# Two small fp32 products of a two-layer token-mixing trunk made from rounded parts: the GLA gate's product in one stacked pass, the heads' mean squares in two passes

## The chip, the cores and the metric

One core of one Trainium2 chip. The metric is the device time of one execution in microseconds (us), the median of three runs.

## The reference, cut to what matters

Two layers over 512 positions of width 1024. Each layer has a token mixer and a convolutional feed-forward part. The mixer projects the normalised input once, runs three groups of heads of width 64 (6 retention, 6 stick-breaking, 4 gated linear attention, "GLA") and projects their outputs. The two products that the change touches are the GLA gate and the mean squares over the 64 columns of a head:

```python
def head_groupnorm(o, g):
    ...
    mu = jnp.mean(o, axis=-1, keepdims=True)
    var = jnp.mean(jnp.square(o - mu), axis=-1, keepdims=True)
    return (o - mu) * lax.rsqrt(var + EPS) * g...
def head_rmsnorm(o, g):
    ...
    return o * lax.rsqrt(jnp.mean(o * o, axis=-1, keepdims=True) + EPS) * g...
def token_mixer(hn, w_in, gla_w2, gla_b, ret_norm_g, gla_norm_g, w_out):
    ...
    ret = merge_heads(head_groupnorm(ret, ret_norm_g)) * jax.nn.silu(rg)
    ...
    log_alpha = jax.nn.log_sigmoid(glr @ gla_w2 + gla_b) / GLA_TAU   # glr: 16 columns
    ...
    go = merge_heads(head_rmsnorm(go, gla_norm_g)) * jax.nn.silu(gg)
    return jnp.concatenate([ret, sb, go], axis=-1) @ w_out
```

All of it is fp32.

## The kernel before, in words

**Products.** Nearly every large product is fp32 made of three passes of a rounded type (fp32r): each operand is split into a rounded part "hi" and the rest "lo", and `mm3` adds hi x hi, hi x lo and lo x hi in PSUM. A weight's split is in `unit`: a DMA into `raw`, ScalarE's cast to `hi` (L361), VectorE's subtraction to `lo` (L362). `split` (L372, L373) does the same for an intermediate result. All matmuls pass through one helper, so their line is L92.

**The mixer of a layer** consists of pieces that are interleaved: the projections of 128 columns (24 fp32r matmuls of 128x512 each, tiles `pj`), a chain for the two GLA pairs of heads, a chain that alternates the three stick-breaking pairs and the three retention pairs (order s0 r0 s1 r1 s2 r2), and steps of the conditioning vector ("ada", L255 on VectorE, one DMA each), which in layer 0 run beside the mixer. A string of letters per layer (TOK) fixes the order in which the program issues pieces. A scheduler makes each engine's final order at build time out of that order and its own account of which inputs will be ready; each engine then runs its own list in that order, and the lists are what the rows of the order below show. The matmuls of `head_rstd` are under `seq("n")` with mode 0, which leaves their place to the scheduler.

**The gate's product.** `use_gv` (L564) takes the 16 columns of the low-rank projection, transposes them to `glrT` (16 x 512) and loads `gla_w2` into `w2` (16 x 256). `gla_pair` multiplies 16x128 of `w2` with `glrT` as one fp32 matmul: two pairs and two layers make four of them. ScalarE and VectorE make the gate from it, and the seven levels of the pair's scores (groups of 32 products of 64x64) follow.

**The mean squares.** `normed` squares a 128x512 output of two heads on ScalarE (L436); `head_rstd` multiplies it with the constant `blk64` (1/64 in two diagonal blocks) as one fp32 matmul (L423 by way of L92) and makes the reciprocal root: Ln and Exp (L226), a correction step (L429 square on ScalarE, L430 on VectorE, L431 on ScalarE), then L439 and L440 on VectorE. Three retention pairs and two GLA pairs in each of two layers make ten of these products.

**A pair of stick-breaking heads** (`sb_head`) starts with scores on TensorE; then, for three tiles, Abs (L780), Exp, Ln, a cast (L785) on ScalarE and two steps on VectorE (L783, L786); more products; Exp. **A retention pair** makes its scores in the same way, multiplies them with decays on VectorE (L827), adds up values on TensorE, and ScalarE copies the result out (L834).

**The end of the mixer.** The last retention pair's and the second GLA pair's mean squares stand next to each other; behind them on TensorE come the matmuls of the output projection `wo`, which begin with the stick-breaking heads' columns, and on ScalarE five Silu gates (L867) between two table loads, and then the first split (L372) of a gated output.

Of the kernel before, what the change touches and what calls it, by code (L numbers as in the profile page):

```python
# [12 lines left out]
F32R = mybir.dt.float32r  # L13
# [3 lines left out]
ALU = mybir.AluOpType  # L17
AX = mybir.AxisListType

P = 128  # L20
S = 512
# [77 lines left out]
def trunk(ctx: ExitStack, tc: tile.TileContext, A, out, dbg=None):  # L99
# [18 lines left out]
    def nm(s):  # L118
        cnt[0] += 1
        return f"{s}_{cnt[0]}"  # L120

    def T(tag="m", shape=(P, 512), dt=F32):
        tag = TMAP.get(tag, tag)
        return tiles[tag].tile(list(shape), dt, tag=tag, name=nm(tag + "_"))
# [4 lines left out]
    def bank(t):  # L129
        t = PMAP[t]  # L130
        return banks[t].tile([P, 512], F32, tag=t, name=nm(t))
# [4 lines left out]
    def psz():  # L136
        return bank("pz")
# [4 lines left out]
    def psg():  # L142
        return bank("pg")

    V, SC, G, PE = nc.vector, nc.scalar, nc.gpsimd, Recorder(nc.tensor)

    @contextmanager
    def seq(kind):

        mode = MODE[kind]  # L150
        m = (None, PE.last, PE.lastp)[mode]
        if m is not None:
            with tc.issue_after(m.ins):
                yield
        else:
            yield
        if kind == "p":
            PE.lastp = PE.last

    lastw = [None]  # L160
    start = {"on": True, "ld": None, "pe": None, "ws": []}

    def ld(t, src, gated=False, kind=None):
        q = QUEUE.get(kind, "sp")
        if q != "sp":
            return (G if q == "g" else SC).dma_start(t, src)


        m = lastw[0] if gated else start["ld"]
        if m is None:  # L170
            r = nc.sync.dma_start(t, src)
        else:
            with tc.issue_after(m.ins):
                r = nc.sync.dma_start(t, src)
        if start["on"]:
            start["ld"] = r
        return r
# [5 lines left out]
    def as32(t):  # L183
        return t.bitcast(F32)


    def const(name, shape, dt=F32, kind=None):
        t = cp.tile(list(shape), dt, tag=name, name=name)
        ld(t, A[name], False, kind)
        return t  # L190
# [33 lines left out]
    def act(*a, **k):  # L224
        with tc.issue_after(tables[0].ins):
            last_act[0] = SC.activation(*a, **k)  # L226
# [143 lines left out]
    def split(ps, th="m", tl="m"):  # L370
        h, l_ = T(th, dt=F32R), T(tl, dt=F32R)
        SC.copy(h, ps)  # L372
        V.tensor_tensor(l_, ps, as32(h), ALU.subtract)  # L373
        return h, l_
# [44 lines left out]
    def head_rstd(sq):  # L419

        ps = psg()
        with seq("n"):
            PE.matmul(ps, C["blk64"], sq, start=True, stop=True)  # L423
        y = T("hl")
        act(y, ps, AF.Ln, bias=epsc, scale=1.0)
        act(y, y, AF.Exp, scale=-0.5)

        t = T("hl")
        SC.activation(t, y, AF.Square)  # L429
        V.scalar_tensor_tensor(t, ps, EPS, t, ALU.add, ALU.mult)  # L430
        SC.activation(t, t, AF.Copy, bias=1.5, scale=-0.5)  # L431
        return y, t

    def normed(o, gcol):
        sq = T("hl")
        SC.activation(sq, o, AF.Square)  # L436
        yield
        y, t = head_rstd(sq)
        V.scalar_tensor_tensor(o, o, gcol, y, ALU.mult, ALU.mult)  # L439
        V.tensor_tensor(o, o, t, ALU.mult)  # L440
# [6 lines left out]
    C = {}  # L447
# [3 lines left out]
    V.memset(C["reset"].rearrange("p (c t) -> p c t", t=CH)[:, :, 0:1], 0.0)  # L451

    def late_consts():
        for n in ("tri", "negones"):
            t = T("hl", (P, P))
            ld(t, A[n])
            C[n] = cp.tile([P, P], F32R, tag=n, name=n)
            V.tensor_copy(C[n], t)
        t = T("hl", (P, P))
        ld(t, A["negm"])  # L460
        C["negm"] = cp.tile([P, P], BF16, tag="negm", name="negmb")
        V.tensor_copy(C["negm"], t)
        C["identb"] = cp.tile([P, P], BF16, tag="identb", name="identb")
        V.tensor_copy(C["identb"], ident)
        C["blk64"] = const("blk64", (P, P))
        C["lev"] = const("lev", (P, len(LEVELS), CH), U32)
        pv[1] = cp.tile([P, NPV], F32, tag="pv1", name="pv1")
        ld(pv[1], A["pv"][1])
# [74 lines left out]
    def mixer(l, hnh, hnl, after):  # L543
# [3 lines left out]
        res = {}  # L547
# [16 lines left out]
        def use_gv(tb, ps):  # L564
            vtok[tb] = T("gv", (P, 272))
            SC.copy(vtok[tb], ps[:, 0:272])
            if tb == NTB - 1:
                w2 = T("gl", (16, 256))
                ld(w2, A["gla_w2"][l], True)
                ps = psg()  # L570
                for t in range(NTB):
                    PE.transpose(ps[0:16, t * P : t * P + P], vtok[t][:, 256:272], ident)
                glrT = T("gl", (16, S))
                SC.copy(glrT, ps[0:16, :])
                res["w2"], res["glrT"] = w2, glrT

        trig, dms = [], {}

# [14 lines left out]
        def project(n):  # L593
            if n[:2] in ("sv", "gv", "rv"):
                src, w, use = {"sv": (A["wsv"], 384, use_sv), "gv": (A["wgv"], 272, use_gv),
                               "rv": (A["wrv"], 384, use_rv)}[n]
                if n in start:
                    for tb, ps in enumerate(start.pop(n)):
                        use(tb, ps)
                else:  # L600
                    yield from proj_tok(src[l], w, hnh, hnl, use)
                res[n] = True
                return
            res[n] = project_T(n[:2], int(n[2]))
            yield
# [284 lines left out]
        for tb in range(NTB):  # L890
            cs = slice(tb * P, tb * P + P)
            ps = psz()
# [76 lines left out]
    if WARM:  # L969

        ps = psz()
# [78 lines left out]
    start["sv"], start["T"] = acc, accT  # L1050
    start["on"] = False
    late_consts()
    crow_d = dp.tile([1, D], F32, tag="crow", name="crow")
    ld(crow_d.rearrange("o (k p) -> (o k) p", p=P), crow)
# [113 lines left out]
```

## Time and profile before

| what | value |
|---|---|
| median of 3 runs | 1392.14 us (1389.92 to 1395.08) |
| the profiled execution's own time | 1393.45 us |
| its span, first to last instruction | 1391.7 us |
| TensorE (PE) busy | 1354.5 us, 97% of the span |
| VectorE (DVE) / ScalarE (ACT) busy | 838.3 us, 60% / 633.3 us, 46% |
| mean granted TensorE clock | 0.995 of full speed |
| fp32r matmuls of the projections | 976 x 3, 392 ns each as recorded |

The recorded time of a matmul is longer than the step from one start to the next, because they overlap in the pipeline; where a matmul's cost is wanted, the starts are compared. A fp32 matmul shows as two records (x2).

### The profile page before, as it was taken

To read this page: it belongs to the slowest core of one execution; us is meant where nothing else is said; L and a number is where in the kernel's file an instruction comes from. 1 tells how busy PE (TensorE), PEld (TensorE's weight loads), DVE (VectorE), ACT (ScalarE), POOL (GpSimd) and SP (SyncE) were. 2 spreads that over 40 slices of the span, in tenths; PEclk is the share of its full clock that TensorE was granted. 3 is DMA by queue.
4 is the path that set the end of the run, shared out by engine and by line. 5 is a ranking of instruction groups with operands and counts; after the bars stand their busy time and mean duration, and the time that the engine had idled before them with its cause. 6 is when DMAs were issued, how large, how long until landed. Compare 5 with 4: busy or idle time off the path is not lost.

```text
span 1391.7 us, 19758 instructions
## 1 busy us (share of the span) xinstructions
PE 1354.5 (97%) x7619; PEld 1110.6 (80%) x7619; DVE 838.3 (60%) x1572; ACT 633.3 (46%) x1033; POOL 54.0 (4%) x97
## 2 busy tenths in 40 slices
PE   8999999999999999999999999999999999999997
PEld 5887667767988888888899877777898888888886
DVE  4559988665888874424563587776565444443232
ACT  5455465765543333322254556675564333332220
POOL 1000000001000000000020000000010000000000
PEclk9999999999999999999999999999999999999999
DMA  9635461204677852233753222111343223222233
GB/s 323 222 119 170 156 210 59 77 32 165 233 254 254 260 187 100 91 105 119 241 172 123 69 92 76 46 62 61 122 151 113 99 92 106 91 98 100 91 106 106
DMA packets 73999, 186.22 MB, mean 134 GB/s; under 512 B 8833, under 2 KB 9905, under 8 KB 73905
## 3 DMA queue, kind: packets, MB, share of 16 engines
q1 hardware_dynamic: 72512, 182.68, 38.9%
q0 software_dynamic: 1088, 2.12, 0.4%
q8 instruction: 60, 0.98, 0.3%
q14 instruction: 35, 0.28, 0.1%
q10 hardware_dynamic: 304, 0.16, 0.1%
HBM read 176.51 MB, written 8.41 MB: 133 GB/s over the span
## 4 chain that ended last, share of the span: by engine, by line
PE 65%; DVE 5%; ACT 3%; DMA 1%; issue 1%; POOL 0%; DVEq 0%; POOLq 0%; SPq 0%; ACTq 0%
PE pj L92 40%; PE ps L92 25%; DVE lo L362 1%; ACT hi L361 1%; DMA m__707_3526<-x 0%; DMA m__1755_9280<-x 0%; DMA raw<-wu 0%; DMA raw<-wT 0%; ACT junk L516 0%; ACT junk L307 0%; POOL s L295 0%; DVE hnl L342 0%; ACT m__1632_8684 L226 0%; DVE m__1675_8921 L742 0%; DVE m__1460_7779 L742 0%
## 5 line engine op out<-in xcount | busy, mean ns | idle before, releaser
L362 DVE TENSOR_TENSOR lo<-raw,hi 128x1024 fp32r<-128x1024 f32 (+2 forms) x208 | 245.7, 1183 | 258.2 <-ACT hi L361 250.0
L92 PE MATMUL pj<-hnh,lo 128*128 128x512 f32 x976 | 382.3, 392 | 2.0 <-DVE lo L362 2.0
L92 PE MATMUL pj<-hnh,hi 128*128 128x512 f32 x976 | 383.6, 393 | 0.0
L92 PE MATMUL pj<-hnl,hi 128*128 128x512 f32 x976 | 382.1, 392 | 0.0
L361 ACT CAST hi<-raw 128x1024 fp32r<-128x1024 f32 (+2 forms) x208 | 211.5, 1018 | 334.9 <-PE pj L92 171.0
L92 PEld LDWEIGHTS pj<-hnh,lo 128*128 128x128 f32 x976 | 183.7, 188 | 40.5 <-DVE lo L362 2.3
L92 PEld LDWEIGHTS pj<-hnh,hi 128*128 128x128 f32 x976 | 183.7, 188 | 39.7 <-issue 2.8
L92 PEld LDWEIGHTS pj<-hnl,hi 128*128 128x128 f32 x976 | 183.6, 188 | 37.7 <-issue 0.8
L255 DVE SCALAR_TENSOR_TENSOR ada<-ada,cB 128x512 f32<-128x512 f32 x160 | 107.2, 686 | 32.1 <-DMA ada<-ada 31.1
L92 PE MATMUL pj<-hi,hnh 128*128 128x384 f32 (+1 forms) x160 | 51.2, 320 | 0.0
L92 PE MATMUL pj<-lo,hnh 128*128 128x384 f32 (+1 forms) x160 | 50.9, 318 | 0.0
L92 PE MATMUL pj<-hi,hnl 128*128 128x384 f32 (+1 forms) x160 | 50.9, 318 | 0.0
L295 POOL TENSOR_TENSOR s<-s,nhalf 128x1 f32<-128x1 f32 x32 | 20.4, 638 | 760.0 <-DVE s L293 756.4
L92 PE MATMUL ps<-hnl,hi 128*128 128x256 f32 x128 | 36.4, 288 | 1.1 <-DVE hnl L342 1.1
L92 PE MATMUL ps<-hnh,lo 128*128 128x256 f32 x128 | 35.8, 284 | 0.0
L92 PE MATMUL ps<-hnh,hi 128*128 128x256 f32 x128 | 35.8, 289 | 0.0
L524 ACT ACTIVATE junk<-ps 128x512 bf16<-128x512 f32 x16 | 9.6, 597 | 51.5 <-PE ps L92 51.3
L92 PEld LDWEIGHTS pj<-hi,hnh 128*128 128x128 f32 x160 | 30.1, 188 | 0.5
L92 PEld LDWEIGHTS pj<-lo,hnh 128*128 128x128 f32 x160 | 30.0, 188 | 0.3
L92 PEld LDWEIGHTS pj<-hi,hnl 128*128 128x128 f32 x160 | 30.1, 188 | 0.0
L92 PEld LDWEIGHTS ps<-hnl,hi 128*128 128x128 f32 x128 | 24.6, 193 | 1.5 <-DVE hnl L342 1.3
L92 PEld LDWEIGHTS ps<-hnh,hi 128*128 128x128 f32 x128 | 24.7, 197 | 0.0
(2786 smaller groups left out, 2485.5 us busy)
## 6 DMA issues: line engine op xcount, KB each, us to landing
raw<-wu SPq DMA_DIRECT2D x88, 512.0 KB, 3.3
ada<-ada SPq DMA_DIRECT2D x160, 256.0 KB, 3.5
raw<-wd SPq DMA_DIRECT2D x44, 512.0 KB, 3.2
raw<-wT SPq DMA_DIRECT2D x42, 512.0 KB, 3.5
raw<-wo SPq DMA_DIRECT2D x16, 512.0 KB, 3.2
raw<-wsv SPq DMA_DIRECT2D x8, 384.0 KB, 3.6
raw<-wrv SPq DMA_DIRECT2D x8, 384.0 KB, 3.1
raw<-wgv SPq DMA_DIRECT2D x8, 272.0 KB, 2.7
```

Of the source, the lines that this page charges most:

```text
L92: self.last = self.e.matmul(*a, **k)
L255: V.scalar_tensor_tensor(raw, raw, 1.0, cB[h], ALU.mult, ALU.mult, accum_out=pt[:, 4 * h + j : 4 * h + j + 1])
L295: G.tensor_tensor(r, v, nhalf, ALU.pow)
L361: SC.copy(h, raw)
L362: V.tensor_tensor(l_, raw, as32(h), ALU.subtract)
L524: SC.activation(junk, ps, AF.Square, accum_out=ss)
```

## The change

The gate's product becomes one fp32r matmul over 128 rows. Two tiles are filled with zeros by GpSimd. `w3` holds the rounded `gla_w2` at partitions 0 and 64 and its rest at 32; `g3` holds the rounded `glrT` at 0 and 32 and its rest at 64, so that one pass adds hi x hi, lo x hi and hi x lo. Per layer this adds two memsets on GpSimd, two copies of 16x256 and two subtractions on VectorE, and one more copy of 16x512 on ScalarE.

The mean squares' product becomes two fp32r passes with the rounded square and its rest. Each of the ten gets a cast (L372, ScalarE) and a subtraction (L373, VectorE) of 128x512. `blk64` is now loaded with `tri` and `negones` through a staging tile and a copy.

```diff
@@ head_rstd
         with seq("n"):
-            PE.matmul(ps, C["blk64"], sq, start=True, stop=True)
+            for i, t in enumerate(split(sq)):
+                PE.matmul(ps, C["blk64"], t, start=(i == 0), stop=(i == 1))
@@ late_consts
-        for n in ("tri", "negones"):
+        for n in ("tri", "negones", "blk64"):
...
-        C["blk64"] = const("blk64", (P, P))
@@ use_gv
-                w2 = T("gl", (16, 256))
+
+                w2, w3, g3 = T("gl", (16, 256)), T("gl", (P, 256), F32R), T("gl", dt=F32R)
+                for t in (w3, g3):
+                    G.memset(as32(t), 0.0)
                 ld(w2, A["gla_w2"][l], True)
+                for r in (0, 64):
+                    V.tensor_copy(w3[r : r + 16, :], w2)
+                V.tensor_tensor(w3[32:48, :], w2, as32(w3[0:16, :]), ALU.subtract)
                 ps = psg()
                 for t in range(NTB):
                     PE.transpose(ps[0:16, t * P : t * P + P], vtok[t][:, 256:272], ident)
-                glrT = T("gl", (16, S))
-                SC.copy(glrT, ps[0:16, :])
-                res["w2"], res["glrT"] = w2, glrT
+                for r in (0, 32):
+                    SC.copy(g3[r : r + 16, :], ps[0:16, :])
+                V.tensor_tensor(g3[64:80, :], ps[0:16, :], as32(g3[0:16, :]), ALU.subtract)
+                res["w2"], res["glrT"] = w3, g3
```

Lines of the changed kernel are one higher from the product in `head_rstd` up to the constants, and seven higher behind `use_gv` (L436 is L437 there, L780 is L787). The scheduler also gives other places to instructions that the diff does not touch.

**First place: TensorE and VectorE at the mean squares of retention pair 0 in layer 0.** In a row stand line, operation, tile written <- tiles read, and shape. `pj_...` is a projection, `ps_1822` (now `ps_1832`) the mean squares, `ps_1833` to `ps_1835` (now `ps_1848` to `ps_1850`) the scores of stick-breaking pair 1. TensorE before:

```order
L92 MATMUL pj_2016<-hnh_116,hi_2012 128x512
L95 MATMUL ps_1745<-ident,m__334_1736 128x128 x4
L92 MATMUL ps_1822<-m__331_1712,blk_654 128x512
L92 MATMUL ps_1833<-m__276_1471,m__313_1641 128x512
L92 MATMUL ps_1833<-m__278_1473,m__313_1641 128x512
```

TensorE now, behind the same transposes, one matmul of `pj_2031` and 20 of `pj_1919` that read `lo_1916` or come after such a one:

```order
L92 MATMUL pj_1919<-hnl_117,hi_1915 128x512
L92 MATMUL pj_1919<-hnh_116,lo_1916 128x512
L92 MATMUL ps_1832<-m__361_1833,blk_650 128x512
L92 MATMUL ps_1848<-m__278_1481,m__315_1651 128x512
L92 MATMUL ps_1848<-m__280_1483,m__315_1651 128x512
L92 MATMUL ps_1849<-m__278_1481,m__315_1651 128x384
L92 MATMUL ps_1849<-m__280_1483,m__315_1651 128x384
L92 MATMUL ps_1850<-m__278_1481,m__315_1651 128x256
L92 MATMUL ps_1850<-m__280_1483,m__315_1651 128x256
L92 MATMUL ps_1849<-m__278_1481,m__315_1651 128x128
L92 MATMUL ps_1832<-m__362_1834,blk_650 128x512
```

VectorE before:

```order
L399 SCALAR_TENSOR_TENSOR m__351_1799<-m__347_1791,m__349_1797 64x512
L399 SCALAR_TENSOR_TENSOR m__352_1800<-m__347_1791,m__350_1798 64x512
L362 TENSOR_TENSOR lo_2013<-raw_2010,hi_2012 128x1024
L255 SCALAR_TENSOR_TENSOR ada_1940,s_1809<-ada_1940,cB_110 128x512
L740 COPY m__339_1752<-ps_1943 64x64 x2
```

VectorE now:

```order
L399 SCALAR_TENSOR_TENSOR m__353_1809<-m__349_1801,m__351_1807 64x512
L399 SCALAR_TENSOR_TENSOR m__354_1810<-m__349_1801,m__352_1808 64x512
L362 TENSOR_TENSOR lo_2028<-raw_2025,hi_2027 128x1024
L373 TENSOR_TENSOR m__362_1834<-m__333_1722,m__361_1833 128x512
L255 SCALAR_TENSOR_TENSOR ada_1955,s_1819<-ada_1955,cB_110 128x512
```

The product of the mean squares stood right behind the transposes; its first pass now stands behind 22 projection matmuls (the 24 of `pj_1919` but for the two that stand ahead of the transposes), the second behind seven of the scores. The new subtraction (L373) stands behind the long L362. The cast that it reads (`m__361_1833`) stands on ScalarE behind the two L398 of the pair's queries.

**Second place: TensorE and ScalarE at the end of the mixer of layer 0.** `ps_3083` and `ps_3094` (now `ps_3108` and `ps_3124`) are the last two mean squares, of GLA pair 1 and of retention pair 2, `ps_3138` (now `ps_3173`) the first tile of the output projection. TensorE before:

```order
L92 MATMUL ps_3083<-m__589_3032,blk_654 128x512
L92 MATMUL ps_3094<-m__604_3081,blk_654 128x512
L92 MATMUL ps_3138<-hi_3144,m__286_1520 128x512
L92 MATMUL ps_3138<-lo_3145,m__286_1520 128x512
L92 MATMUL ps_3138<-hi_3144,m__287_1521 128x512
```

TensorE now:

```order
L92 MATMUL ps_3108<-m__614_3109,blk_650 128x512
L92 MATMUL ps_3108<-m__615_3110,blk_650 128x512
L92 MATMUL ps_3124<-m__619_3125,blk_650 128x512
L92 MATMUL ps_3173<-hi_3179,m__288_1530 128x512
L92 MATMUL ps_3173<-lo_3180,m__288_1530 128x512
L92 MATMUL ps_3173<-hi_3179,m__289_1531 128x512
L92 MATMUL ps_3124<-m__620_3126,blk_650 128x512
```

ScalarE before:

```order
L834 COPY m__603_3079<-ps_3070 128x512
L436 ACTIVATE m__604_3081<-m__603_3079 128x512
L226 ACTIVATE m__606_3085<-ps_3083,epsc 128x512
L226 ACTIVATE m__606_3085<-m__606_3085 128x512
L429 ACTIVATE m__607_3088<-m__606_3085 128x512
L226 ACTIVATE m__609_3096<-ps_3094,epsc 128x512
L226 ACTIVATE m__609_3096<-m__609_3096 128x512
L431 ACTIVATE m__607_3088<-m__607_3088 128x512
```

ScalarE now:

```order
L841 COPY m__611_3104<-ps_3095 128x512
L437 ACTIVATE m__612_3106<-m__611_3104 128x512
L372 CAST m__614_3109<-m__597_3057 128x512
L226 ACTIVATE m__616_3115<-ps_3108,epsc 128x512
L226 ACTIVATE m__616_3115<-m__616_3115 128x512
L430 ACTIVATE m__617_3118<-m__616_3115 128x512
L372 CAST m__619_3125<-m__612_3106 128x512
L432 ACTIVATE m__617_3118<-m__617_3118 128x512
L226 ACTIVATE m__621_3131<-ps_3124,epsc 128x512
```

The cast for the second product (`m__619_3125`) has come to stand behind Ln, Exp and the square (L430) that the first product's result goes through, and TensorE has the second product's first pass ahead of the output projection.

**Third place: TensorE at the mean squares of retention pair 1 in layer 0.** Before, the product follows the 32 small products of a GLA level. Now the last of the small products is followed by 11 projection matmuls, the last of which stands first here:

```order
L92 MATMUL pj_2817<-hnh_116,lo_2814 128x512
L92 MATMUL ps_2627<-m__520_2628,blk_650 128x512
L92 MATMUL ps_2643<-m__433_2226,m__441_2269 128x512
L92 MATMUL ps_2643<-m__435_2228,m__441_2269 128x512
L92 MATMUL ps_2644<-m__433_2226,m__441_2269 128x384
```

Ahead of the small products stand 14 projection matmuls that before stood behind them: the scores of stick-breaking pair 2 (`ps_2643` to `ps_2645`) have moved behind 25 matmuls of 128x512.

## Rows read from the trace of the kernel before

**Rows 1.** The page of the profile: the span, the first line of part 1 (busy time of each engine, its share of the span, its instructions) and the first line of part 4 (share of the chain of waits that ended last, by engine).

```profile
span 1391.7 us, 19758 instructions
...
PE 1354.5 (97%) x7619; PEld 1110.6 (80%) x7619; DVE 838.3 (60%) x1572; ACT 633.3 (46%) x1033; POOL 54.0 (4%) x97
...
PE 65%; DVE 5%; ACT 3%; DMA 1%; issue 1%; POOL 0%; DVEq 0%; POOLq 0%; SPq 0%; ACTq 0%
```

**Rows 2.** The timeline of TensorE at the first gate product of layer 0. Columns: start in us, busy us, engine, line, operation, tile written <- tiles read, shape, and in brackets the idle time just before it with what ended it.

```profile
84.38 0.39 PE L92 MATMUL pj<-hnh,lo 128*128 128x512 f32 x1
84.69 1.12 PE L92 MATMUL ps<-m__163_870,m__161_863 16*128 16x512 f32 x2
...
86.08 0.40 PE L92 MATMUL pj<-hnl,hi 128*128 128x512 f32 x1
```

**Rows 3.** The timeline of TensorE at the mean squares of retention pair 0 in layer 1; same columns.

```profile
844.37 0.40 PE L92 MATMUL pj<-hnh,hi 128*128 128x512 f32 x1
844.60 1.12 PE L92 MATMUL ps<-m__1456_7769,blk 128*128 128x512 f32 x2
...
845.79 0.39 PE L92 MATMUL ps<-m__1416_7577,m__1442_7695 128*128 128x512 f32 x1
```

**Rows 4.** The timeline of TensorE around the mean squares of retention pair 0 in layer 0; same columns.

```profile
157.53 0.63 PE L95 MATMUL ps<-ident,m__334_1736 128*128 128x128 f32 x4 [0.23 <-DVE m__334_1736 L709]
157.99 1.02 PE L92 MATMUL ps<-m__331_1712,blk 128*128 128x512 f32 x2
...
160.41 0.50 PE L92 MATMUL pj<-hnh,lo 128*128 128x512 f32 x1
...
165.32 0.39 PE L92 MATMUL pj<-hnh,lo 128*128 128x512 f32 x1
...
169.24 0.50 PE L92 MATMUL pj<-hnh,lo 128*128 128x512 f32 x1 [2.01 <-DVE lo L362]
```

**Rows 5.** The timeline of ScalarE (ACT) at the same place; same columns.

```profile
163.49 1.29 ACT L398 ACTIVATE m__349_1797<-m__347_1791 64x512 fp32r<-64x512 f32 x2 [4.71 <-DVE m__347_1791 L590]
164.79 1.28 ACT L398 ACTIVATE m__350_1798<-m__347_1791 64x512 fp32r<-64x512 f32 x2
166.10 0.69 ACT L226 ACTIVATE m__359_1824<-ps,epsc 128x512 f32<-128x512 f32 x1
```

**Rows 6.** The timeline of VectorE (DVE) at the same place; same columns.

```profile
159.14 1.22 DVE L362 TENSOR_TENSOR lo<-raw,hi 128x1024 fp32r<-128x1024 f32 x1
...
167.96 1.23 DVE L362 TENSOR_TENSOR lo<-raw,hi 128x1024 fp32r<-128x1024 f32 x1
```

**Rows 7.** The timeline of TensorE at the mean squares of retention pair 1 in layer 0: the 32 small products of the GLA level just before them; same columns.

```profile
243.71 0.69 PE L92 MATMUL ps<-m__499_2528,m__498_2527 64*64 64x64 f32 x32
```

**Rows 8.** The timeline of ScalarE there, from the square of retention pair 1 to the first step of stick-breaking pair 2; same columns.

```profile
243.11 0.63 ACT L436 ACTIVATE m__502_2544<-m__501_2542 128x512 f32<-128x512 f32 x1
...
247.61 0.39 ACT L780 ACTIVATE m__519_2633<-ps 128x256 f32<-128x256 f32 x1
...
251.16 1.05 ACT L361 CAST hi<-raw 128x1024 fp32r<-128x1024 f32 x1 [0.78 <-PE pj L92]
```

**Rows 9.** [...]

```profile
169.83:173.24 3.41, 3.41 (x10) 2.61 (x8) 3.33 (x9) 1.91 (x4) 0.00 (x0) 0.50 0.64 231
247.60:272.10 24.50, 23.29 (x175) 18.56 (x173) 14.79 (x25) 19.20 (x35) 1.04 (x2) 1.00 0.16 55
272.10:282.40 10.30, 7.71 (x42) 6.17 (x44) 7.82 (x13) 7.26 (x13) 1.00 (x2) 1.00 0.25 93
282.47:285.88 3.41, 3.41 (x18) 1.55 (x16) 2.10 (x8) 0.00 (x0) 0.00 (x0) 0.50 0.48 159
```

**Rows 10.** The timeline of TensorE at the end of the mixer of layer 0, from the last mean squares into the output projection; columns as in Rows 2.

```profile
296.06 1.13 PE L92 MATMUL ps<-m__604_3081,blk 128*128 128x512 f32 x2 [0.28 <-ACT m__604_3081 L436]
296.62 0.79 PE L92 MATMUL ps<-hi,m__286_1520 128*128 128x512 f32 x1
...
306.73 0.50 PE L92 MATMUL ps<-hi,m__611_3112 128*128 128x512 f32 x1
```

**Rows 11.** The timeline of ScalarE at the same place; same columns.

```profile
295.38 0.63 ACT L436 ACTIVATE m__604_3081<-m__603_3079 128x512 f32<-128x512 f32 x1
295.92 0.67 ACT L226 ACTIVATE m__606_3085<-ps,epsc 128x512 f32<-128x512 f32 x1
296.62 0.63 ACT L226 ACTIVATE m__606_3085<-m__606_3085 128x512 f32<-128x512 f32 x1
297.28 0.63 ACT L429 ACTIVATE m__607_3088<-m__606_3085 128x512 f32<-128x512 f32 x1
...
306.06 0.62 ACT L372 CAST m__611_3112<-m__411_2092 128x512 fp32r<-128x512 f32 x1
```

**Rows 12.** The timeline of VectorE at the end of the mixer of layer 1: one subtraction of a split; same columns.

```profile
978.86 0.69 DVE L373 TENSOR_TENSOR m__1705_9057<-m__1509_8057,m__1704_9056 128x512 fp32r<-128x512 f32 x1 [0.83 <-ACT m__1704_9056 L372]
```

**Rows 13.** The timeline of TensorE at the end of the mixer of layer 1; same columns.

```profile
966.77 1.13 PE L92 MATMUL ps<-m__1688_8994,blk 128*128 128x512 f32 x2
968.22 1.12 PE L92 MATMUL ps<-m__1697_9025,blk 128*128 128x512 f32 x2 [0.32 <-ACT m__1697_9025 L436]
968.78 0.79 PE L92 MATMUL ps<-hi,m__1419_7596 128*128 128x512 f32 x1
...
978.88 0.50 PE L92 MATMUL ps<-hi,m__1704_9056 128*128 128x512 f32 x1
```

## The prediction

> **What bounds the kernel now.** The page comes first: TensorE is busy 1354.5 of 1391.7 us, and it has 65% of the chain of waits [rows 1]. So a microsecond of matmul taken away is a microsecond won, as long as TensorE then has something ready; some 37 us of idle time is all there is. Next the timeline of TensorE shows what the two products cost. Then the stretches: in the mixer of layer 0 TensorE is not full everywhere. [...] The change takes work from TensorE and puts two steps, a cast and a subtraction, in front of each mean square; so the question is at each of the ten places what TensorE does until they are done, and the order of the engines answers it.
>
> **Part 1, the gate's product, four times.** From the projection matmul before it to the second one behind it the starts lie 86.08 - 84.38 = 1.70 us apart [rows 2]. Projection matmuls follow each other at 4.91 / 21 = 0.23 us, 22 of them from 160.41 to 165.32 [rows 4]. So the product costs 1.70 - 2 x 0.23 = 1.24 us. One rounded pass of 512 columns costs 0.23, with some 0.06 that a change of destination may add (84.38 to 84.69 is 0.31): 0.95 us saved, **4 x 0.95 = 3.8 us**. What is added beside it (memsets, copies of 16 rows, one subtraction) belongs to the first pair's preparation, with whole projections between it and its use; I cost it at nothing. Without that cover, the chain of one copy and one subtraction would cost about 1.3 us a layer.
>
> **Part 2, the mean squares, ten times.** 845.79 - 844.37 - 2 x 0.23 = 0.96 us for the fp32 product [rows 3], against two passes at 0.46: 0.50 us saved, **10 x 0.50 = 5.0 us**. The two passes are seen to cost 0.23 at this very shape, so I leave no wide bound here. [...] Together: **-8.8 us** if nothing waits.
>
> **Part 3, retention pair 0 of layer 0.** Behind the transposes (157.53 + 0.46) and one matmul, TensorE comes to `lo_1916` at 158.2; the subtraction that writes it runs from 159.14 [rows 6], and the first matmul that needed it started at 160.41 [rows 4]. Before, the mean squares and the scores filled that time; now they stand behind: 2.2 us idle. 22 matmuls later, at 165.5, the first pass needs its cast, which stands on ScalarE behind L398, over at 164.79 + 1.28 = 166.07 [rows 5]; with 0.62 for the cast, as at 306.06 [rows 11], 166.7: 1.2 us idle. The second pass, at 168.1, needs the subtraction behind the L362 that starts at 167.96 and takes 1.14 until the next can start; with 0.69 for itself [rows 12] it is there at 169.8: 1.7 us. That makes 5.1. The 2.01 us that TensorE waited at 169.24 [rows 4] go, since that operand is now there in time. **+3.1 us.** Bounds: nothing, if VectorE gets to its work earlier; 5.1.
>
> **Part 4, retention pair 1 of layer 0.** 14 matmuls now come ahead of the small products that started at 243.71 [rows 7]: 246.9. These take 0.6, two more matmuls end a projection at 248.1, and there ScalarE gets its next weight's cast (1.05 [rows 8]), a copy of about 0.6 and then the cast of the square: 250.3. TensorE arrives at 250.1. Scores and passes take about 2, Ln, Exp and the square 2.0 [rows 11]: the Abs of stick-breaking pair 2, at 247.61 before [rows 8], comes at about 254.2, 6.6 us later, while TensorE has done 25 x 0.23 = 5.8 us of its filling work beforehand. If that chain can't be shortened, the end of the mixer moves by 6.6; if TensorE sets the pace again, by nothing. Over the stretch TensorE was busy 92% [rows 9], and the chain waited for it in places; I take the middle, **+3.5 us**.
>
> **Part 5, the ends of the two mixers.** Layer 0: the square of the last output is done at 296.0, the cast of the first comes behind it, 295.92 to 296.5 [rows 11]. Pass one at 296.6, subtraction to 297.2, pass two to 297.7. Then ScalarE's Ln, Exp and square, 0.70, 0.66 and 0.54 from start to start: 299.6. Only there the second cast can start, to 300.2, and pass one of the second product stands on TensorE ahead of the output projection, whose first matmul thus starts at 300.5, against 296.62 [rows 10]. The gated output that TensorE took at 306.73 is then ready at about 310.1, by the same steps, and wanted at 310.6, so no new wait arises there. **+3.9 us.** For layer 1 the same order from 966.77 gives the output projection at 972.65 against 968.78 [rows 13], again +3.9. Since 1.0 of the savings of part 2 lie in each, this is 4.9 of waiting each, **+9.8 us**. The rule behind it: an instruction whose inputs are ready waits when one ahead of it on its engine does. The Ln at 166.10 shows it: its product was made from 157.99 on, and it started when the L398 ahead of it were over [rows 4, 5]. [...] If ScalarE could take the cast earlier instead, this part would be +0.9 each and the whole change would be faster.
>
> **Part 6, the other four products** (GLA pair 0 in both layers, retention pairs 0 and 1 in layer 1) are also moved, behind 11 to 35 projection matmuls, so that cast and subtraction are mostly covered; what is late next is the start of a stick-breaking or GLA chain, by 2 to 3 us, with less filling work left. Nearest row: part 3, 3.1. Bounds 0 and 3.1 each; I take 0.7, because in layer 1 no ada steps stand ahead: **+2.8 us**.
>
> **Sum.** -8.8 + 3.1 + 3.5 + 9.8 + 2.8 = **+10.4 us**. The profiled execution (1393.45, of which 1391.7 is the span) is 1.3 above the median; put on the median 1392.1 this gives **1402.5 us**, slower by 0.75%.
>
> **Rivals.**
> - *Faster: TensorE stays the bound.* The waits are taken up by projection matmuls, as 97% busy suggests, and the saving remains: 1392.1 - 8.8 = 1383.3. It decides the case if the waits add up to less than 1.8 us, since 8.8 - 1.8 = 7 us (0.5%) is about what a measurement of this kernel can tell from no change. For it: the share of 97% [rows 1]. Against it: at the ends no other matmul stands between the passes. 0.11.
> - *No change: ends only.* Parts 3, 4 and 6 are covered, the ends are not: -8.8 + 9.8 = +1, 1393; up to part 3 with it, 1396. 0.25.
> - *Much slower: the late chains.* Parts 4 and 6 at their upper bounds: -8.8 + 3.1 + 6.6 + 9.8 + 12.4 = +23, 1415; a further half-clock stretch of 3.41 us, as the two in [rows 9], costs 1.7 each. 0.12.
> - *The rounded passes cost what the fp32 product costs*, and nothing is saved: 1411. The rows of 0.23 speak against it; within the slower cases, 0.02.
>
> **The numbers.** Forecast and its neighbours (1399 to 1412) 0.50, with the two slower rivals 0.64 for slower by over 0.5%; same 0.25; faster 0.11. The range 1387 to 1413 leaves out the faster case and the top of the slowest.
>
> **What would show it.** Right: in the changed profile the output projection of each mixer starts about 4 us later behind the last stick-breaking or retention values than before, TensorE idle between two passes of mean squares there; idle before L92 `lo` and two waits for L372 and L373 at retention pair 0; gate products with one record of 0.39. Wrong: TensorE's busy time falls by about 9 and its idle time does not grow, or the idle time grows elsewhere than at these casts and subtractions.

## The result, and the profile after

| | before | changed |
|---|---|---|
| median of 5 runs | 1392.47 us | 1413.38 us (1412.66 to 1416.01) |
| ratio | | 1.0141, 95% interval 1.012 to 1.0163 |
| span of the profiled execution | 1391.7 us | 1414.2 us |
| mean granted clock there | 0.995 | 0.98 |

Slower by 1.4%, some 20 us; the forecast was slower by 10. The median of these five, 1413.38, is 0.4 us above the 1413 at which the stated range ends; the ratio put on the forecast's 1392.1 us gives 1411.7, inside its top. The execution that was profiled is the slowest of the five (1416.01; its clock of 0.98 is the lowest, the others have 0.982 to 0.987), so its trace shows somewhat more than the median. The page of the changed kernel, lines as in [rows 1]:

```profile
span 1414.2 us, 19802 instructions
...
PE 1366.9 (97%) x7615; PEld 1124.4 (80%) x7615; DVE 848.0 (60%) x1591; ACT 639.4 (45%) x1045; POOL 55.3 (4%) x101
...
PE 56%; DVE 8%; DMA 6%; ACT 3%; issue 1%; POOL 0%; DVEq 0%; POOLq 0%; ACTq 0%; SPq 0%
```

TensorE has less to do and is busy 12.4 us *longer*; its share of the chain of waits fell from 65% to 56%, VectorE's rose from 5% to 8% and that of DMA from 1% to 6%. These shares don't tell where the time went: DMA's new share is the conditioning vector's transfers in layer 0's feed-forward part, and what lies between the two mixers is only 1.2 us longer. Where it happened is seen in two stretches of either kernel, each up to the first matmul of an output projection: the mixer of layer 0 from 140 us on, and all from the start of the feed-forward part's last product in layer 0 (its first 126 us are the same in all these traces) to layer 1's output projection. The columns, as in [rows 9], are the stretch and its length in us, the busy us and the instructions of PE, PEld, DVE, ACT and POOL, TensorE's granted clock as a share of full speed, the DMA share and GB/s. Before:

```profile
140.00:296.62 156.62, 144.59 (x1041) 107.71 (x1040) 124.73 (x263) 88.80 (x151) 6.55 (x12) 0.98 0.35 115
593.88:968.78 374.90, 368.81 (x2316) 301.53 (x2314) 227.29 (x427) 186.14 (x320) 18.65 (x31) 1.00 0.32 107
```

Changed:

```profile
140.00:309.22 169.22, 149.82 (x1041) 114.14 (x1040) 129.45 (x270) 92.74 (x158) 6.75 (x12) 0.91 0.32 106
607.72:991.11 383.39, 372.64 (x2312) 305.67 (x2311) 232.90 (x438) 190.50 (x328) 19.36 (x33) 0.99 0.31 104
```

Layer 0: 156.62 to 169.22, +12.6 us; TensorE is idle 19.4 us in place of 12.0 (length less busy time) and busy 5.2 longer at a mean clock of 0.91. Layer 1: +8.5; idle 10.75 in place of 6.09. Together 21.1 of the 22.5 us by which the spans differ; what follows each mixer is nearly as long as before. The half-clock stretches (granted 0.50 or 0.51 of full speed) in the mixer of layer 0, of which before there were two of 3.41 us [rows 9]:

```profile
160.63:164.04 3.41, 3.41 (x8) 2.76 (x9) 3.39 (x7) 0.37 (x1) 0.00 (x0) 0.51 0.95 330
181.02:191.25 10.23, 10.10 (x47) 8.66 (x48) 7.69 (x17) 5.01 (x10) 0.00 (x0) 0.50 0.84 266
279.97:293.60 13.63, 7.07 (x30) 4.92 (x31) 7.51 (x16) 5.68 (x10) 0.99 (x2) 0.50 0.16 60
307.30:314.10 6.80, 5.48 (x13) 4.37 (x14) 3.39 (x5) 4.75 (x8) 0.00 (x0) 0.50 0.00 0
```

34 us at half clock, and TensorE busy in 26 of them. In the second TensorE was busy but for 0.13 us, and no idle time just ahead of it is longer than 0.73; the first, third and fourth lie behind or around idle time of 2.02, 5.67 and 2.61 us, shown below.

### The profile page after: what moved, and what is told of

Same layout as the page of the kernel before. It is cut to its first block, busy times and chain, and to the rows that moved or that the text cites. A ratio compares the mean times of both kernels' runs of the same rounds, so it can differ in the third digit from the quotient of the medians.

```text
span 1414.2 us, 19802 instructions
## 1 busy us (share of the span) xinstructions
PE 1366.9 (97%) x7615; PEld 1124.4 (80%) x7615; DVE 848.0 (60%) x1591; ACT 639.4 (45%) x1045; POOL 55.3 (4%) x101
## 4 chain that ended last, share of the span: by engine, by line
PE 56%; DVE 8%; DMA 6%; ACT 3%; issue 1%; POOL 0%; DVEq 0%; POOLq 0%; ACTq 0%; SPq 0%
PE pj L92 32%; PE ps L92 25%; DMA ada<-ada 6%; DVE lo L362 2%; DVE ada L255 1%; ACT hi L361 1%; DMA m__719_3561<-x 0%; DMA m__1823_9538<-x 0%; DMA raw<-wT 0%; DVE hnl L342 0%; DVE m__1340_7120 L708 0%; DVE m__1694_8979 L749 0%; DVE m__1472_7821 L749 0%; DVE m__1473_7822 L749 0%; DVE s L558 0%
## 5 line engine op out<-in xcount | busy, mean ns | idle before, releaser
L362 DVE TENSOR_TENSOR lo<-raw,hi 128x1024 fp32r<-128x1024 f32 (+2 forms) x208 | 245.7, 1183 | 249.0 <-ACT hi L361 245.8
```

Of the source, the lines that this page charges most:

```text
L362: V.tensor_tensor(l_, raw, as32(h), ALU.subtract)
```

## The places of the prediction, in the trace after

The first gate product, TensorE, columns as in [rows 2]:

```profile
85.58 0.39 PE L92 MATMUL pj<-hnh,lo 128*128 128x512 f32 x1
85.81 0.39 PE L92 MATMUL ps<-m__164_867,m__163_866 128*128 128x512 f32 x1
86.04 0.39 PE L92 MATMUL pj<-hnh,hi 128*128 128x512 f32 x1
```

One record, and the next matmul starts 0.23 us later, as far apart as the projection's pass before it (85.58) and the product (85.81): the product costs what a projection's pass costs, 0.06 less than forecast.

Retention pair 0 in layer 0, TensorE, to set against [rows 4]:

```profile
157.71 0.63 PE L95 MATMUL ps<-ident,m__336_1746 128*128 128x128 f32 x4 [0.24 <-DVE m__336_1746 L716]
...
160.59 0.80 PE L92 MATMUL pj<-hnh,lo 128*128 128x512 f32 x1 [2.02 <-DVE lo L362]
...
167.30 0.40 PE L92 MATMUL ps<-m__361_1833,blk 128*128 128x512 f32 x1
167.53 0.39 PE L92 MATMUL ps<-m__278_1481,m__315_1651 128*128 128x512 f32 x1
...
168.84 0.50 PE L92 MATMUL ps<-m__362_1834,blk 128*128 128x512 f32 x1
```

The wait of 2.02 us for `lo` stands where it was expected (2.2). The other two, for the cast and the subtraction, do not: TensorE, at half clock from 160.63 to 164.04 (granted 0.51), came to its first pass at 167.30 and found the cast done. The run ends_fp32 (below) has the same order here, and in its trace the clock is full at this place (granted 1.00 from 158 to 163 us); there all three waits come, the last two at 1.03 and 0.21 us (forecast 1.2 and 1.7):

```profile
158.94 0.50 PE L92 MATMUL pj<-hnh,lo 128*128 128x512 f32 x1 [2.02 <-DVE lo L362]
...
165.30 0.50 PE L92 MATMUL ps<-m__361_1833,blk 128*128 128x512 f32 x1 [1.03 <-ACT m__361_1833 L372]
...
167.13 0.50 PE L92 MATMUL ps<-m__362_1834,blk 128*128 128x512 f32 x1 [0.21 <-DVE m__362_1834 L373]
```

Retention pair 1 in layer 0, ScalarE, from the new cast to the Abs of stick-breaking pair 2, to set against [rows 8]:

```profile
250.08 0.62 ACT L372 CAST m__520_2628<-m__508_2564 128x512 fp32r<-128x512 f32 x1
252.97 0.69 ACT L226 ACTIVATE m__522_2634<-ps,epsc 128x512 f32<-128x512 f32 x1 [2.27 <-PE ps L92]
...
254.89 0.37 ACT L787 ACTIVATE m__527_2658<-ps 128x256 f32<-128x256 f32 x1
```

254.89 where it was 247.61 (forecast: 254.2). What comes of it is seen on TensorE at the transposes of GLA pair 1, before and now:

```profile
280.58 0.63 PE L95 MATMUL ps<-ident,m__569_2892 128*128 128x128 f32 x4 [1.86 <-DVE m__569_2892 L709]
```

```profile
288.24 1.09 PE L95 MATMUL ps<-ident,m__577_2917 128*128 128x128 f32 x4 [5.67 <-DVE m__577_2917 L716]
```

+7.7 us, and 5.67 us idle ahead of it: none of the delay was made up. The delay is not the order's alone. Half-clock stretches of 3.41, 3.41 and 10.24 us stand ahead of this Abs in the changed kernel's trace; with the same order and no such stretch ahead (granted 1.00 from 140 to 250 us) it is at 251.18 (ends_fp32, below), 3.6 us later than before and not 7.3.

The end of layer 0's mixer on TensorE, to set against [rows 10]:

```profile
304.79 0.50 PE L92 MATMUL ps<-m__614_3109,blk 128*128 128x512 f32 x1 [1.84 <-ACT m__614_3109 L372]
305.52 0.50 PE L92 MATMUL ps<-m__615_3110,blk 128*128 128x512 f32 x1 [0.23 <-DVE m__615_3110 L373]
308.62 0.80 PE L92 MATMUL ps<-m__619_3125,blk 128*128 128x512 f32 x1 [2.61 <-ACT m__619_3125 L372]
309.22 0.63 PE L92 MATMUL ps<-hi,m__288_1530 128*128 128x512 f32 x1
```

and on ScalarE, to set against [rows 11]:

```profile
302.99 0.58 ACT L841 COPY m__611_3104<-ps 128x512 f32<-128x512 f32 x1 [4.34 <-PE ps L92]
...
304.14 0.60 ACT L372 CAST m__614_3109<-m__597_3057 128x512 fp32r<-128x512 f32 x1
306.05 0.69 ACT L226 ACTIVATE m__616_3115<-ps,epsc 128x512 f32<-128x512 f32 x1 [1.31 <-PE ps L92]
...
307.97 0.60 ACT L372 CAST m__619_3125<-m__612_3106 128x512 fp32r<-128x512 f32 x1
```

The copy of the last output at 302.99, the cast for the first product at 304.14, Ln at 306.05, and only at 307.97 the cast for the second, for which TensorE waits 2.61 us; the output projection starts at 309.22. From that copy to the output projection it is 6.23 us, and was 296.62 - 294.76 = 1.86 before. The copy before, in layer 0 and in layer 1:

```profile
294.76 0.59 ACT L834 COPY m__603_3079<-ps 128x512 f32<-128x512 f32 x1 [4.33 <-PE ps L92]
...
966.92 0.59 ACT L834 COPY m__1696_9023<-ps 128x512 f32<-128x512 f32 x1 [1.66 <-PE ps L92]
```

In layer 1 it was 966.92 to 968.78 [rows 13], also 1.86, and is now 984.88 to 991.11, again 6.23:

```profile
984.88 0.58 ACT L841 COPY m__1715_9081<-ps 128x512 f32<-128x512 f32 x1 [2.65 <-PE ps L92]
```

```profile
991.11 0.63 PE L92 MATMUL ps<-hi,m__1432_7639 128*128 128x512 f32 x1
```

## The experiments

Ratios are to the kernel before on the same chip, with 95% intervals. The kernel before took 1392.5 us beside the changed kernel and 1394.4 to 1395.5 in the three series below, and executions of it within one series spread over 8 to 10 us; so a time is to be read by its ratio, and a microsecond between the stretches of two traces proves nothing by itself. In every run the scheduler also makes another order. Diffs are cut to their main lines; lines marked - and + are against the changed kernel, unless said otherwise. Theory W: the loss is the waits for the new casts and subtractions and the half clock behind them. It was put to the test first, together with the saving itself.

**gate_only**: the changed kernel with the mean squares as before (`blk64` is loaded as before too).

```diff
-            for i, t in enumerate(split(sq)):
-                PE.matmul(ps, C["blk64"], t, start=(i == 0), stop=(i == 1))
+            PE.matmul(ps, C["blk64"], sq, start=True, stop=True)
```

> Only the gate's product is changed; the mean squares stay one fp32 product. Theory W (TensorE waits at the new casts and subtractions of the mean squares, and runs at half clock after these waits): nothing of that is here, the four gate products save 3.8 us, so about 1388.7 us, 1387 to 1391. Rival G (the gate's extra steps or the order that they bring take part in the loss): 1393 or more.

Measured 1393.25 us against 1394.41, ratio 0.9987 (0.9973 to 1.0002). The 1393.25 taken alone would lie in rival G's "1393 or more"; beside the 1394.41 of the same series it is no loss. The gate has no part in the loss, so rival G falls. How much of its 3.8 us comes out the interval leaves open (-3.8 to +0.3 us, 1.8 at its middle).

**ms_only**: the kernel before with the mean squares' part of the change alone (the diff of `head_rstd` and `late_consts`).

> Only the mean squares are changed. Theory W: the whole loss is here and the gate's saving is missing: about 1413.4 + 3.8 = 1417 us, and idle time and half-clock stretches as in the changed kernel. Rival G: under 1408.

Measured 1415.33, ratio 1.0163 (1.0131 to 1.0194). The whole loss is in the mean squares.

**one_pass**: no split at all.

```diff
-            for i, t in enumerate(split(sq)):
-                PE.matmul(ps, C["blk64"], t, start=(i == 0), stop=(i == 1))
+            PE.matmul(ps, C["blk64"], sq, start=True, stop=True)
...
-        sq = T("hl")
+        sq = T("hl", dt=F32R)
```

> As the changed kernel, but ScalarE writes the square rounded and one rounded pass makes the mean square: the rest (the lo part) of the square is left out of the sum, and there is no cast and no subtraction. Theory W: no wait is added, so TensorE's saving comes out in full: 3.8 + 10 x 0.73 = 11.1 us, about 1381.5 us, 1379 to 1385. Rival S (the loss comes from the other order that the scheduler makes, whatever the waits): 1390 or more.

Measured 1397.77, ratio 1.0025 (1.0012 to 1.0038): 11 us of matmul less by the prices of the prediction, no wait added, and 3 us *slower*. Theory W was wrong on this: the saving does not come out. The time is in rival S's region (1390 or more), and no run separates rival S, since each has an order of its own; the clock, median 0.991 against 0.996 of the kernel before in this series, also bears on it (see the paragraph on the clock below). The two stretches of this kernel, as above:

```profile
140.00:296.46 156.46, 139.62 (x1032) 106.31 (x1031) 124.51 (x262) 87.66 (x149) 6.46 (x11) 0.97 0.35 115
594.41:969.85 375.44, 368.38 (x2308) 302.64 (x2307) 228.28 (x431) 186.15 (x320) 19.36 (x33) 0.99 0.33 107
```

From 140 us to layer 0's output projection TensorE is busy 139.62 us in place of 144.59, and the stretch is 156.46 long in place of 156.62: 5 us of saved work became 5 us of idle time. In the second stretch, at a mean granted clock of 0.99 (before 1.00), TensorE's busy time hardly falls (368.38 from 368.81) and the length is 0.5 us greater.

**ms_twice**: the kernel before with its fp32 product issued a second time.

```diff
+            PE.matmul(ps, C["blk64"], sq, start=True, stop=True)
             PE.matmul(ps, C["blk64"], sq, start=True, stop=True)
```

> The kernel before with each of the ten fp32 mean-square products issued twice (the second overwrites the first): 10 x 0.96 = 9.6 us of TensorE time more, no new wait on another engine. Theory K (the mixers' length is set by the chain through ScalarE and VectorE, and TensorE time saved there turns into idle time): most of the 9.6 is taken up by idle time except at the two ends, where two products each stand on the path: +2 to +5 us, 1396 to 1399. Rival P (TensorE is the bound, the saving of the rounded products came out and something else ate it): +9 us or more, 1403.

Measured 1396.33, ratio 1.001 (0.9993 to 1.0026). 9.6 us of matmul more cost 1 us (-1.0 to +3.6), less than theory K had it:

```profile
140.00:295.87 155.87, 147.61 (x1053) 109.27 (x1052) 126.04 (x265) 89.51 (x152) 7.00 (x12) 0.99 0.35 115
594.54:971.93 377.39, 373.18 (x2325) 303.47 (x2324) 227.22 (x427) 186.13 (x320) 18.36 (x31) 1.00 0.32 106
```

In the mixer of layer 0 TensorE is busy 3 us more and the stretch is 0.75 shorter. So in layer 0, where TensorE was busy 92% (144.59 of 156.62), the mixer's length is seen from both sides not to be set by TensorE's work on these products. In layer 1 (busy 98% of that stretch) it is less clear: the doubled work made the stretch 2.5 us longer, half of its 4.8. Over the whole kernel rival P falls.

**split_early**: cast and subtraction issued with the square.

```diff
-            for i, t in enumerate(split(sq)):
+            for i, t in enumerate(sq):
...
         SC.activation(sq, o, AF.Square)
+        sq = split(sq)
         yield
```

> As the changed kernel, but the square is split right behind the squaring, ahead of the point where the chain hands over, so that cast and subtraction are issued earlier; the same instructions in number. Theory W: the casts no longer stand behind Ln, Exp and the square at the mixers' ends, the waits there fall from 4.7 to about 2 us each, those at the retention pairs go mostly: 1385 to 1392 us. Rival C (the two added steps on the chain cost that much wherever they stand): 1403 or more.

Measured 1404.86, ratio 1.0088 (1.0057 to 1.0119): theory W's 1385 to 1392 is missed, and the time is in rival C's region (1403 or more). But the places W names did change. The end of layer 0 on ScalarE, the copy of the last output and the cast of its square:

```profile
299.49 0.58 ACT L842 COPY m__613_3108<-ps 128x512 f32<-128x512 f32 x1 [6.01 <-PE ps L92]
...
300.77 0.62 ACT L372 CAST m__615_3112<-m__614_3110 128x512 fp32r<-128x512 f32 x1
```

and on TensorE the pass that waits for it and the output projection:

```profile
301.44 0.50 PE L92 MATMUL ps<-m__615_3112,blk 128*128 128x512 f32 x1 [1.55 <-ACT m__615_3112 L372]
301.78 0.39 PE L92 MATMUL ps<-hi,m__288_1530 128*128 128x512 f32 x1
```

The cast no longer stands behind Ln, Exp and square: from copy to output projection 2.3 us, not 6.2. In layer 1 it is 2.3 too. Placing gives about 7 of 20 us back; the rest stays. Whether the added steps cost that rest wherever they stand, as rival C has it, the runs that leave them out have to tell.

**ends_fp32**: the last two mean squares of each mixer as before, the other six split.

```diff
-            for i, t in enumerate(split(sq)):
+            for i, t in enumerate((sq,) if last else split(sq)):
-                PE.matmul(ps, C["blk64"], t, start=(i == 0), stop=(i == 1))
+                PE.matmul(ps, as32(C["blk64"]) if last else C["blk64"], t, start=(i == 0), stop=last or (i == 1))
```

(`last` is true for GLA pair 1 and retention pair 2.)

> The changed kernel, but the last two mean squares of each mixer (GLA pair 1 and retention pair 2) stay one fp32 product without a cast and a subtraction. Theory W (waits at the ends): the output projection follows the last copy by 1.9 us as before, not by 6.2, and with the half-clock stretches behind these waits gone 10 to 13 us come back: 1400 to 1404. Rival E (the loss comes from the chain inside the mixer, the ends are hidden): 1409 or more.

Measured 1401.97, ratio 1.0053 (1.0033 to 1.0074): 12 us of the 20 come back (1.0141 - 1.0053 = 0.0088 of 1393; with both intervals, 8 to 16); rival E falls. On TensorE and ScalarE:

```profile
299.28 1.13 PE L92 MATMUL ps<-m__597_3057,blk 128*128 128x512 f32 x2
300.69 1.13 PE L92 MATMUL ps<-m__612_3106,blk 128*128 128x512 f32 x2 [0.28 <-ACT m__612_3106 L437]
301.25 0.79 PE L92 MATMUL ps<-hi,m__288_1530 128*128 128x512 f32 x1
```

```profile
299.39 0.59 ACT L841 COPY m__611_3104<-ps 128x512 f32<-128x512 f32 x1 [4.33 <-PE ps L92]
```

The copy is at 299.39, so 1.86 us to the output projection, as before. The waits at the two ends are 2 x 4.4 = 8.8 of the 12. The profiled execution is the fastest of the eight (1398.45, the median is 1401.97). Its Abs of stick-breaking pair 2:

```profile
251.18 0.37 ACT L787 ACTIVATE m__527_2658<-ps 128x256 f32<-128x256 f32 x1
```

**ends_ro1_fp32**: retention pair 1 of layer 0 as before too (`last` is true for it as well).

> The changed kernel, with the last two mean squares of each mixer and that of retention pair 1 in layer 0 as one fp32 product. Theory K (what is left of the loss without the ends, some 7 us, is mostly the later start of stick-breaking pair 2 in layer 0): the Abs of that pair comes 2.5 to 3.5 us earlier than with the ends alone, and the time falls by as much: 1398 to 1400 us. Rival D (the rest is spread over the other products): 1401 or more.

Measured 1395.95 against 1395.51, ratio 1.0004 (0.9989 to 1.0018): level, by the ratios 6.8 us better than with the ends alone, and better than the 1398 to 1400 expected; rival D falls. The Abs:

```profile
247.12 0.39 ACT L787 ACTIVATE m__525_2653<-ps 128x256 f32<-128x256 f32 x1
```

4.1 us earlier, where 2.5 to 3.5 were expected. The five mean squares that still take two passes, with their casts and subtractions, and the gate together cost and give nothing outside the interval (-1.5 to +2.5 us). So rival C of split_early, that the added steps cost wherever they stand, does not hold for these five.

**early_ends_fp32**: the ends as before, the other six split early (both diffs above).

> The changed kernel, with the last two mean squares of each mixer as one fp32 product and the other six split right behind the squaring, ahead of the hand-over. Theory W+K (the loss is the waits at the ends and the late starts inside, both by the places of cast and subtraction, and the saved matmul time turns into idle time): neither is here, so it is level with the kernel before, 1393 to 1397 us against 1395, not 7 us faster. Rival P (TensorE's saving comes out once the waits are gone: 3.8 + 6 x 0.5): 1388 or less. Rival C (the added steps cost wherever they stand): 1400 or more.

Measured 1397.94, ratio 1.0025 (1.0008 to 1.0043). Neither rival's time; slower by 3.5 us by the ratio, clear of level, and 0.9 us above the 1393 to 1397 that W and K gave. No run shows where these 3.5 us are. Early placing serves no better than the single fp32 product at retention pair 1.

**fill_l0**: the changed kernel with filler products ahead of GLA pair 1's transposes in layer 0.

```diff
             with seq("g"):
+                for _ in range(22 * (j == 1 and l == 0)):
+                    PE.matmul(ps, C["reset"][:, 0:P], C["reset"], start=True, stop=True)
                 for tb in range(NTB):
```

> The changed kernel with 22 bf16 products of 128x512 into a bank that is overwritten later, issued on TensorE where it waits for the last stick-breaking pair and for GLA pair 1 in layer 0 (4.7 us of matmul in 8 us of idle time). Theory H (half clock behind idle time costs time of its own): the half-clock stretches from 280 to 294 go or shrink and 3 to 5 us come back: 1409 or less. Rival K (that stretch is set by the chain on ScalarE and VectorE, so the clock there is hidden): 1412 to 1416; if the fillers are in the way, more.

Measured 1416.16, ratio 1.0162 (1.0135 to 1.0188), as the changed kernel. The fillers did not cover the wait:

```profile
283.94 0.88 PE L95 MATMUL ps<-ident,m__577_2917 128*128 128x128 f32 x4 [3.40 <-DVE m__577_2917 L718]
```

The scheduler put them between 269 and 276 us; 3.40 us of the 5.67 stay idle. Theory H wanted the half-clock stretches to shrink: by its mean clock of 0.986 the profiled execution ran (1 - 0.986) x 2 x 1417 = 40 us at half clock, where the changed kernel's ran 57 by its 0.98, but no time came back. Where in this trace the 40 us stand is not shown, so this tells little on the clock.

**gate_fill**: gate_only with ten such fillers.

> The kernel before with the stacked gate product alone and 10 such filler products ahead of GLA pair 1's transposes in layer 0. Theory H: the half-clock stretch from 282 goes, 1.7 us on top of what the gate saves: about 1390 us. Rival: no difference from the gate alone, 1393.

Measured 1390.02 against 1395.27, ratio 0.997 (0.9959 to 0.9982): the one version that beats both kernels, by 0.3%. Its profiled execution has no half-clock stretch at 282 us (granted 1.00 from 281 to 285), where the kernel before has one [rows 9]; from 140 to 294.58 us its mean granted clock is 0.99. Its interval and that of gate_only overlap, so how much of it is the fillers' is not settled.

## Why the prediction was right, and where it was off

**The direction and the places hold, the size of the terms only in part.** The steps in front of the mean squares cost more than the passes save, at the places named: the ends of both mixers and retention pair 1 of layer 0. Without those five products' splits the loss is gone (1.0004), without the gate nothing of it changes. How the loss divides between the waits, the changed order and the clock is shown for the ends alone, and there in part.

**Parts 1 and 2, -8.8 us: the sum's failed term.** The price of a product was right (0.23 per pass). But the sum took every microsecond off TensorE as won, and the prediction's first sentences say why: TensorE's 97%. Over the kernel that is not so: 11 us of matmul less gave nothing (one_pass), 9.6 more cost 1 us (ms_twice). In layer 0 the saving is seen turned into idle time; that a chain on ScalarE and VectorE sets the length there is the reading that fits, not one that a run shows by itself. With this term at 0 in place of -8.8 the same sum gives +19.2, against 20 measured. That the other terms add up so well is partly luck, as follows.

**Part 3, +3.1.** In the changed kernel's trace one of three waits came (2.02 us), TensorE being late itself at half clock for the others. At full clock (ends_fp32, granted 1.00 from 158 to 163 us) all three came, 2.02, 1.03 and 0.21, 3.3 us in all where 5.1 were summed up, and less the 2.01 that went, 1.3 and not 3.1; the wait for the subtraction was the one mis-sized. By ends_ro1_fp32, which has this place unchanged, it costs nothing in the end that can be told.

**Part 4, +3.5 taken, 0 to 6.6 bounds.** The late start agrees (254.89 against 254.2) by luck: about half of it came with the half-clock stretches, which the working has not, and at full clock (granted 1.00 from 140 to 250 us) the same order gives 251.18, 3.6 us late where 6.6 were worked out. The choice of the middle was wrong in its reason: all of the delay was carried to the transposes, +7.7 at 254.89 and in ends_fp32 +4.0 at 251.18, and undoing it gave 6.8 us (3.3 to 10 with both intervals). The reason was that TensorE is 92% busy there and would set the pace again; that is the same error as in parts 1 and 2, and [rows 9] give 89% for the two stretches from 247.6 to 282.4 (31.00 of 34.80 us).

**Part 5, +3.9 for each end.** Measured +4.4 each, from the copy to the output projection. Instructions that wait behind others on ScalarE were walked correctly. What lies above it, some 3.5 of the 12 us that ends_fp32 gave back, is within the noise, and may go with half-clock stretches: the changed kernel's trace has such stretches from 307, 362, 980 and 990 us, and that of ends_fp32 has room for one of 3.41 us at most: its mean clock of 0.994 makes (1 - 0.994) x 2 x 1397 = 17 us of half clock, 13.6 of them from 276.6 to 290.2 (granted 0.50). But those from 24, 161, 181 and 884 are as good as gone by this too, and these ends don't explain them.

**Part 6, +2.8.** Nothing that the interval can tell: ends_ro1_fp32 keeps these four products and retention pair 0's, and is level.

**The rivals.** "TensorE stays the bound" was wrong at its root. "Ends only" was short by retention pair 1. "Much slower" gave nearly the right number (+23) from a wrong place, the upper bounds of part 6. The half-clock stretches, priced there at 1.7 us apiece, came in greater number: by the mean clocks, (1 - 0.98) x 2 x 1414 = 57 us of them in the changed trace against (1 - 0.995) x 2 x 1392 = 14 before.

**The clock, which the sum left out.** The spans differ by 22.5 us; TensorE's idle time (span less busy time) grew by 10.1 of them, from 37.2 to 47.3, and the other 12.4 are busy time of an engine with less to do. The prediction has waits alone, +19.2 of them. What the half clock is worth no run isolates, but the executions on record give an estimate. For the kernel before, a straight line through time against time at half clock (worked out as above for each execution) has a slope of 0.22, 0.27 and 0.37 us per us in the three series of 19, 27 and 20 executions; in the series of 27 the fastest, 1390.10 us, had a mean clock of 0.998 and the slowest, 1400.51, one of 0.988. The changed kernel's median clock of 0.985 against 0.995 means some 28 us more at half clock, so 6 to 10 of the 20 us. The same estimate puts 3 to 5 us on the 14 us that one_pass has more, which is all that it is slower; its saving still does not come out. This is a correlation: waits and half clock come together, so the two are not separate shares of the loss.

## What to carry to other kernels

A high busy share does not make an engine the bound of a stretch, as layer 0's mixer shows, where TensorE was busy 92%: before a saving is credited, look for the idle time that the stretch already has and what ends it, and ask whether doubling the work would be noticed; one run with the product issued twice answers it, stretch by stretch (here 0 of layer 0's and half of layer 1's extra work was noticed). A split of an operand on other engines is paid where its steps queue (here 4.4 us at the end of each mixer): walk each engine's list in order at the last product before a hand-over, where nothing else is left to run.

## What was not expected of the hardware

The same instructions in the same order, up to about 252 us, ran in different times as the clock went: the Abs of stick-breaking pair 2 stands at 254.89 in the changed kernel's trace, with half-clock stretches of 3.41, 3.41 and 10.24 us ahead of it, and at 251.18 in that of ends_fp32, whose granted clock is full there (1.00 from 140 to 250 us). An idle time of 2.02 us at 160.6 came with such a stretch in the one (160.63 to 164.04 above), and one as long (2.02, at 158.9) without it in the other (granted 1.00 from 158 to 163 us).
